# Batched matmul on one core: whole transposes one step ahead, and y loaded two batches per DMA

## The chip, the cores and the metric

One core of one Trainium2 chip. The metric is the device time of one execution in microseconds. Beside it each run gives the core's span (first to last instruction in the records) and the mean clock granted to TensorE.

## The reference

```python
batch, dim_i, dim_j, dim_k = 32, 256, 512, 384      # float32 in and out
out = np.einsum('bij,bjk->bik', x, y)
```

x is 16.8 MB, y 25.2 MB, out 12.6 MB: 54.5 MB to move. The multiplication itself is done in float16 with float32 sums.

## The kernel before

Two batches (G = 2) make a step u, four (Q = 4) a group q of x. One x load of 2 MiB serves two steps. Every load and store is issued from SyncE, in program order (`keep(...)` holds an instruction at its place in the program). The x tiles are transposed on TensorE against an identity (256 transposes), copied out of PSUM as float16 by VectorE and ScalarE, and used as weights.

```python
    def load(u):
        # ... x of the next group, every second step
        y_of[u] = y_pool.tile([P, G, NJ, K], F32, name="y_sb")     # 5 buffers
        for g in range(G):
            keep(nc.sync.dma_start(
                out=y_of[u][:, g],
                in_=y[u * G + g].rearrange("(q t) k -> q t k", q=P)))   # 0.75 MiB, rows of 6,144 bytes

    # ... transpose(q, half): 16 PE transposes, 2 copies on each of VectorE and ScalarE
    # ... round_y(u): 8 casts; multiply(u): 32 matmuls; collect(u): 4 copies out of PSUM

    ahead = LAG - 2                     # LAG = 4
    for u in range(ahead):
        load(u)
    for s in range(U + 2):              # U = 16 steps
        if s + ahead < U:
            load(s + ahead)
        if s == 0:
            transpose(0, 0); transpose(0, 1)
        if s >= 2:
            collect(s - 2)
        if 1 <= s <= U:
            multiply(s - 1)
        if s < U:
            round_y(s)
        for half in range(2):           # first half in step 2q-1, second in step 2q
            q = (s + 1 - half) * G // Q
            if (s + 1 - half) * G % Q == 0 and 0 < q < B // Q:
                transpose(q, half)
        if s >= 2:
            store(s - 2)
```

## Time and profile before

| | before |
|---|---|
| device time, three runs | 135.94, 135.94, 136.25 us |
| span of the profiled run | 134.3 us |
| busiest compute engine | PE, 66% of the span |
| share of the DMA queue | 97.8% |
| last landing of a y batch, issue of the last store, its landing | 124.1, 129.1, 133.4 us |

The page's list of DMA issues tells the shape of the traffic (name, queue, count, size of one, median time from issue to landing):

```profile
y_sb<-in_y_dram SPq DMA_DIRECT2D x32, 768.0 KB, 17.9
x_sb<-in_x_dram SPq DMA_DIRECT2D x8, 2048.0 KB, 20.8
out_dram<-o_sb SPq DMA_DIRECT2D x16, 768.0 KB, 17.8
```

### The profile page before, as it was taken

The page shows a single profiled execution, that of the slowest core. Times are in us where ns is not written, and L with a number is a line of the kernel's source. Part 1 is how long each engine was busy: PE and PEld are TensorE (multiplying, and loading weights), DVE is VectorE, ACT ScalarE, POOL GpSimd, SP SyncE. Part 2 cuts the span into 40 slices and gives each one's busy share as a digit, 9 for nine tenths or more (in the row PEclk, how much of TensorE's full clock was granted, in tenths as well). Part 3 has the DMA queues.
Part 4 walks back from the last instruction along what each step waited for, and adds up shares of the span by engine and source line. Part 5 has one row for each costly group of instructions (what it writes and reads, how often), then busy time and mean ns, then how long its engine had stood idle before and what let it go on. Part 6 is the DMA issues. An engine that isn't in the chain of part 4 may idle for free.

```text
span 134.3 us, 1968 instructions
## 1 busy us (share of the span) xinstructions
PE 88.5 (66%) x768; PEld 73.2 (55%) x768; DVE 56.2 (42%) x128; ACT 63.9 (48%) x129; POOL 0.7 (1%) x6
## 2 busy tenths in 40 slices
PE   0049494979299767786099771976439986597920
PEld 0049474768177666666078661864427665476810
DVE  0004717471743365711634318460363425628620
ACT  3004837662762476712744428560475336738610
POOL 2000000000000000000000000000000000000000
PEclk9999999999959999999968999999965899779997
DMA  5999999999999999999999999999999999999993
GB/s 112 415 400 450 409 417 421 456 388 421 417 448 408 409 428 421 457 394 417 413 443 436 408 417 428 442 422 402 425 423 444 426 402 427 419 427 419 417 394 158
DMA packets 8073, 54.65 MB, mean 407 GB/s; under 512 B 896, under 2 KB 896, under 8 KB 7040
## 3 DMA queue, kind: packets, MB, share of 16 engines
q1 hardware_dynamic: 8064, 54.53, 97.8%
q8 instruction: 6, 0.10, 0.3%
q14 instruction: 3, 0.02, 0.0%
HBM read 41.94 MB, written 12.58 MB: 406 GB/s over the span
## 4 chain that ended last, share of the span: by engine, by line
DMA 78%; PE 13%; ACT 4%; DVE 0%; issue 0%
DMA y_sb<-in_y_dram 40%; DMA x_sb<-in_x_dram 38%; PE o_ps L130 9%; PE t_ps L99 3%; ACT xt_sb L107 2%; ACT y_r L116 1%; ACT o_sb L143 1%; DVE o_sb L145 0%
## 5 line engine op out<-in xcount | busy, mean ns | idle before, releaser
L130 PE MATMUL o_ps<-y_r,xt_sb 128*64 128x384 f16 x512 | 52.4, 364 | 28.5 <-ACT o_sb L143 20.8
L130 PEld LDWEIGHTS <-xt_sb 128*64 128x64 f16 x512 | 39.1, 121 | 38.8 <-issue 22.4
L116 ACT CAST y_r<-y_sb 128x384 f16<-128x384 f32 x64 | 29.5, 514 | 38.7 <-DMA y_sb<-in_y_dram 38.6
L99 PE MATMUL t_ps<-identity,x_sb 128*128 128x128 f32 x256 | 36.9, 301 | 11.4 <-DMA x_sb<-in_x_dram 11.4
L99 PEld LDWEIGHTS t_ps<-identity,x_sb 128*128 128x128 f32 x256 | 34.1, 211 | 16.0 <-issue 16.0
L118 DVE CAST y_r<-y_sb 128x384 f16<-128x384 f32 x64 | 20.0, 356 | 46.7 <-DMA y_sb<-in_y_dram 46.7
L107 ACT CAST xt_sb<-t_ps 128x512 f16<-128x512 f32 x32 | 22.4, 731 | 23.6 <-PE t_ps L99 23.6
L105 DVE CAST xt_sb<-t_ps 128x512 f16<-128x512 f32 x32 | 22.6, 728 | 24.1 <-PE t_ps L99 23.8
L145 DVE COPY o_sb<-o_ps 128x384 f32<-128x384 f32 x32 | 16.3, 544 | 2.1 <-PE o_ps L130 2.1
L143 ACT COPY o_sb<-o_ps 128x384 f32<-128x384 f32 x32 | 13.9, 492 | 1.3 <-PE o_ps L130 1.3
L107 ACT ACT_TABLE_LOAD x1 | 1.3, 1283 | 0.7 <-PEq L192 0.7
masks.py:199 POOL TENSOR_SCALAR_AFFINE_SELECT identity<-identity 128x128 f32<-128x128 f32 x1 | 0.3, 294 | 0.1
masks.py:197 POOL MEMSET identity<- 128x128 f32 x1 | 0.2, 206 | 0.3 <-POOLq L192 0.3
L192 POOL MEMSET const-bfloat16-1.0<- 128x1 bf16 x1 | 0.1, 102 | 0.0
L192 POOL MEMSET const-uint8-127<- 128x1 uint8 x1 | 0.1, 102 | 0.0
L192 POOL MEMSET const-float32-0.0<- 128x1 f32 x1 | 0.1, 99 | 0.2 <-issue 0.2
L192 POOL MEMSET const-float32-1.0<- 128x1 f32 x1 | 0.1, 99 | 0.0
## 6 DMA issues: line engine op xcount, KB each, us to landing
y_sb<-in_y_dram SPq DMA_DIRECT2D x32, 768.0 KB, 17.9
x_sb<-in_x_dram SPq DMA_DIRECT2D x8, 2048.0 KB, 20.8
out_dram<-o_sb SPq DMA_DIRECT2D x16, 768.0 KB, 17.8
```

The lines of the kernel that those rows point to most:

```text
L99: nc.tensor.transpose(t_ps[:, f, h], x_sb[:, h * NE + e + f, t::NJ], identity)
L105: keep(nc.vector.tensor_copy(dst, t_ps))
L107: keep(nc.scalar.copy(dst, t_ps))
L116: keep(nc.scalar.copy(yr_of[u][:, g, t], y_sb[:, g, t]))
L118: keep(nc.vector.tensor_copy(yr_of[u][:, g, t], y_sb[:, g, t]))
L130: nc.tensor.matmul(o_ps[g * M : (g + 1) * M], xt_sb[:, t, e, a * PQ : (a + 1) * PQ].rearrange("c p h -> c (p h)"), y_r[:, g, t], start=(t ...
L143: keep(nc.scalar.copy(o_of[u][:, e], ps_of[u][e]))
L145: keep(nc.vector.tensor_copy(o_of[u][:, e], ps_of[u][e]))
L192: nc = _bacc.Bacc("TRN2", target_bir_lowering=False, num_devices=1)
```

## The change

The intent was to issue fewer and larger loads, and to have all of a group's transposes done a step before they are needed, so that none stands between two multiplications.

```diff
-        for g in range(G):
+        n = 1 if u == U - 1 else G
+        for g in range(0, G, n):
+            b = u * G + g
             keep(nc.sync.dma_start(
-                    out=y_of[u][:, g],
-                    in_=y[u * G + g].rearrange("(q t) k -> q t k", q=P),
+                    out=y_of[u][:, g : g + n],
+                    in_=y[b : b + n].rearrange("g (q t) k -> q g t k", q=P),
 ...
-        for half in range(2):
-            q = (s + 1 - half) * G // Q
-            if (s + 1 - half) * G % Q == 0 and 0 < q < B // Q:
-                transpose(q, half)
+        if (s + 1) * G % Q == 0 and s + 1 < U:
+            transpose((s + 1) * G // Q)
```

(Cut: `transpose(q)` now loops over all NJ tiles; step 0 calls it once.)

More of the change, by code (lines that the diff above doesn't have):

```diff
@@ L78, in load, with transpose @@
         y_of[u] = y_pool.tile([P, G, NJ, K], F32, name="y_sb")
-        for g in range(G):
+        n = 1 if u == U - 1 else G
+        for g in range(0, G, n):
+            b = u * G + g
             keep(
                 nc.sync.dma_start(
-                    out=y_of[u][:, g],
-                    in_=y[u * G + g].rearrange("(q t) k -> q t k", q=P),
-                )
-            )
-    def transpose(q, half):
-        x_sb = x_of[q]
-        if half == 0:
-            xt_of[q] = xt_pool.tile([P, NJ, NE, Q * PQ, H], MM_DT, name="xt_sb")
+                    out=y_of[u][:, g : g + n],
+                    in_=y[b : b + n].rearrange("g (q t) k -> q g t k", q=P),
+                )
+            )
+    def transpose(q):
+        x_sb = x_of.pop(q)
+        xt_of[q] = xt_pool.tile([P, NJ, NE, Q * PQ, H], MM_DT, name="xt_sb")
         n = 0
-        for t in range(half * NJ // 2, (half + 1) * NJ // 2):
+        for t in range(NJ):
             for e in range(0, NE, 2):
@@ L163 @@
         if s == 0:
-            transpose(0, 0)
-            transpose(0, 1)
+            transpose(0)
         if s >= 2:
```

## The prediction

> **What bounds the kernel now.** I read the page from the top: the busy shares, then the slices, then the DMA queue, then the chain that ended last, and last the SyncE queue and the end of the timeline.
>
> ```profile
> PE 88.5 (66%) x768; PEld 73.2 (55%) x768; DVE 56.2 (42%) x128; ACT 63.9 (48%) x129; POOL 0.7 (1%) x6
> ...
> DMA  5999999999999999999999999999999999999993
> ...
> DMA packets 8073, 54.65 MB, mean 407 GB/s; under 512 B 896, under 2 KB 896, under 8 KB 7040
> ...
> q1 hardware_dynamic: 8064, 54.53, 97.8%
> ...
> DMA 78%; PE 13%; ACT 4%; DVE 0%; issue 0%
> ```
>
> No compute engine is busy over 66% of the span; the 16 DMA engines are busy in every slice but the first and the last, and the packets of the one queue take 97.8% of them. So the kernel is bound by moving 54.5 MB. The chain says only 78% DMA because at two places it walks through compute that releases a store; that is not idle DMA, as the slices there still read 9.
>
> The next view asks what the queue of transfers itself waits for (the waits of the SyncE queue):
>
> ```profile
> SPq L81 <- DMA x_sb<-in_x_dram: 32.8, 7, 5.4
> SPq L150 <- DVE o_sb L145: 20.3, 5, 7.1
> SPq L81 <- DMA y_sb<-in_y_dram: 19.7, 13, 1.5
> SPq L150 <- DMA y_sb<-in_y_dram: 16.7, 11, 1.6
> ```
>
> Loads of y (L81) wait for earlier transfers of x and y, and half of the waiting stores (L150) do too. The listing of the built program shows why: each transfer takes one of eight semaphores in turn, and the ninth waits until the first has landed. So eight transfers are in flight, and the page's 17.9 us from issue to landing of y is the length of that queue: eight transfers of 0.97 MB on average (54.5 MB / 56) at 420 GB/s are 18.5 us. The queue is long, and that is good: nothing runs dry.
>
> The end of the timeline (start, length, engine and line) shows the drain:
>
> ```profile
> 123.51 1.77 ACT L116 CAST y_r<-y_sb 128x384 f16<-128x384 f32 x4
> 124.15 0.63 DVE L118 CAST y_r<-y_sb 128x384 f16<-128x384 f32 x2 [0.28 <-DMA y_sb<-in_y_dram]
> ...
> 128.44 0.56 DVE L145 COPY o_sb<-o_ps 128x384 f32<-128x384 f32 x1 [0.74 <-PE o_ps L130]
> ```
>
> The last batch of y lands at 124.15, the last result is copied out at 129.0, the span ends at 134.3. Five stores (11 to 15 in program order) come after that last load: 5 x 0.786 MB / 420 GB/s = 9.4 us, and 124.15 + 9.4 = 133.5. So the DMA drains without a gap of note to the end.
>
> [...] 896 packets under 512 B are 56 transfers x 16. [...] A y load here is 0.75 MiB and becomes 1.5 MiB. [...] with eight queued, slices already run at 388 to 457 GB/s. [...] the packet records of the trace give 234 ns (median) for a 6,144-byte packet and 9 ns for a semaphore write, so a batch of y is 8 x 234 + 9 = 1.88 us on its engine, and the landings of stores and y batches in the end phase are 1.8 to 1.9 us apart[...].
>
> **The change part by part.**
> *y in pairs.* 32 loads become 17 (15 pairs, and two single ones at the end). Bytes, 6,144-byte rows and the order of x, y and stores on the SyncE queue stay. Removed: 15 semaphore writes per engine, 15 x 9 ns = 0.135 us, on the bound; and 15 issues of 0.33 us, 5 us of SyncE's time, which nothing waits for. Also eight transfers now hold more bytes (54.5 / 41 = 1.33 MB each), so the eight semaphores stop being the limit of the queue and the stores' waits become it. Check that the queue cannot run dry: a y load is issued once the store five steps of y before it in program order is ready. By the timeline that store follows its own multiply; I put it at most 6 us after the landing of the next pair of y, four steps before the load in question lands. A step moves 54.5 / 16 = 3.4 MB, 8.2 us; four steps are 33 us, less 6, less 3.7 for the load itself, leaves over 20 us of work queued ahead. No gap.
> Against it: a pair lands as one, so the casts of its first batch start about 1.9 us later; ACT must then do four casts (4 x 0.514 = 2.06 us) after the landing and not two (1.03): +1.0 us on the compute side of a step.
> *Transposes.* 256 transposes, 64 copies out of PSUM: same count, same sizes, so nothing is removed. The second half of a group of four batches moves from just before its own multiply to one step earlier, so odd steps carry 32 transposes and 8 copies, even ones none. In an odd step, 16 more transposes (2.2 us) and two more copies on each of ACT and DVE (2 x 0.73) stand between the casts and the collecting of the last result: some 2 us later there. In the next step the same 2.2 us + 0.7 us wait is gone. x has landed well before, as it is queued ahead of that step's y. Compute per two steps stays 88.5 / 8 = 11 us of PE against 16.4 us of DMA.
> *The tail.* Before, at 119.95 the last 16 transposes hold multiply 14 up until 123.01. After, by the durations of that timeline: pair 13 lands at 113.0, four ACT casts to 115, copies and transposes to about 117.8, first collect copy 118.3, multiply 13 to 121.0 (2.75 us at full clock) or 122.8 (4.47 us, as that stretch had), multiply 14 behind it, multiply 15 from about 125.1, when the last y is rounded, to 127.8. So the last store is issued near 128.4 where it was 129.1. But the DMA has stores 11 to 14 to move until 131.6 anyway, so those 0.7 us are hidden, but for the small dip in the queue just before 129.1, worth 0.1 us at most.
> *Sum.* The densest reading of the trace: x of the first group lands at 8.59 us; then 48 transfers of 1.881 us and seven of x at 8 x 611 + 9 ns = 4.90 us make 124.6 us, so 133.2, and the last landing, read from the semaphore records, is 133.4. There is 0.2 us of slack in the whole kernel. After the change: -0.135 -0.05 (chosen) gives about -0.2 us: 135.94 becomes **135.75 us**.
>
> **The rivals.**
> (a) *Fewer, larger DMAs are really faster* [...]: if each removed transfer saved a bubble of 0.2 us, 3 us, 133 us. Against: 1.88 us per batch is the sum of its packets; no room for a bubble.
> (b) *The tail turns compute-bound*: with PE at half clock through multiplies 13 to 15 (4.47 us each) the last would end near 131 to 132, the last store be issued at 132 and land some 3.5 us later: 135.5 for the span in place of 134.3, so 137.1. For it: the granted clock was 0.76 from 113 to 120 us. Against: from 120 to 134 it was near full, and the denser transposes come earlier.
> (c) *Pairs read two places of y in turn, 0.79 MB apart*, in place of one run; packets could get slower. 1% more per y packet is 0.6 us. Nothing in the trace speaks for it, as packet length is unchanged; it could go either way.
> (d) *A dry queue at the start*: store 0 now comes after all transposes of group 1, about 26 us in place of 23.9. By then 13 loads (now 8) of 14.2 MB are queued, good until 35 us. No loss.
>
> **Range and chances.** The runs of before differ by 0.3 us (135.94 to 136.25); (c) and the noise give about 0.5 either way, (b) a thin tail upward: 135.2 to 136.4. Over 2% either way means more than 2.7 us: only (a) or a strong form of (b) or (c) reach it. Same 0.96, faster 0.02, slower 0.02.
>
> **What would show it.** Packets under 512 B fall from 896 to 656; the queue's share stays near 98%; the median y landing grows from 17.9 us to over 20; SyncE's waits of L81 on earlier transfers shrink and its stores' waits on o_sb grow; the last y still lands at about 124; no slice of DMA between the first and the last two falls under 9. I am wrong if slices show holes (b, d), or if 6,144-byte packets have another median than 234 ns (a, c).

Its sum: -0.135 -0.05 = -0.185 us, so 135.94 becomes 135.75. What its figures rest on: the 420 GB/s is the rate in the trace (414 to 431 GB/s in each stretch from 8.6 to 127 us). The 56 landings fall on eight semaphores in turn, seven on each; the first transfer landed at 8.59 us and the ninth was issued at 8.60. The trace has 896 packets of 4 bytes, and as many increments of these eight semaphores: the "semaphore writes". The multiply of 4.47 us ran at a mean clock of 0.62 (116 to 120 us), so not at half clock throughout; a multiply at full clock took 2.79 us there, where the forecast estimates 2.75. The bubble of 0.2 us in rival (a) and the 3.5 us from issue to landing in rival (b) were assumptions; later runs measured 3.6 and 3.2 us for the second.

## The result, and the profile after

The changed kernel took **136.50 us** (median of six, 136.30 to 136.72) and the kernel before, in six runs (the three above among them), 136.22 us (135.94 to 136.33). The ratio is 1.0024, 95% interval 1.0009 to 1.0039: the same within 2%, as forecast, but 0.1 us above the range of 135.2 to 136.4, and on the slow side of 1 where the prediction was on the fast side. Ratios here are the mean time of one kernel's fast runs over that of the other's of the same rounds, so not quite the ratio of the medians quoted.

The page after, the lines that answer to those of the prediction (DMA busy by slice, packets, the queue's share, the chain that ended last):

```profile
PE 88.7 (66%) x768; PEld 76.1 (57%) x768; DVE 56.2 (42%) x128; ACT 62.4 (46%) x129; POOL 0.7 (1%) x6
...
DMA  5999999999999999999999999999999999999993
...
DMA packets 7833, 54.64 MB, mean 407 GB/s; under 512 B 657, under 2 KB 657, under 8 KB 6801
...
q1 hardware_dynamic: 7824, 54.53, 97.7%
...
DMA 72%; PE 11%; DVE 6%; SPq 3%; issue 2%; ACT 1%; DVEq 0%; ACTq 0%
```

Nothing that bounds the kernel moved. The 240 small packets that went from the queue (8,064 to 7,824) are 15 transfers x 16 semaphore writes; the bytes, the mean rate of 407 GB/s and the full slices are the same.

What SyncE's queue waits for, after:

```profile
SPq L152 <- DVE o_sb L147: 91.7, 16, 17.5
SPq L84 <- DMA x_sb<-in_x_dram: 4.6, 4, 1.7
SPq L202 <- DMA out_dram<-o_sb: 4.1, 1, 4.1
```

and the list of issues, after:

```profile
y_sb<-in_y_dram SPq DMA_DIRECT2D x15, 1536.0 KB, 24.3
...
y_sb<-in_y_dram SPq DMA_DIRECT2D x2, 768.0 KB, 18.7
```

The loads hardly wait for an earlier transfer any more; the stores wait for their results instead, 91.7 us in all. This large change of who waits for whom cost nothing, because the queue stays 24 us long. The end of the timeline after:

```profile
118.90 5.50 PE L132 MATMUL o_ps<-y_r,xt_sb 128*64 128x384 f16 x64 [0.40 <-DVE o_sb L147]
...
124.27 0.63 DVE L120 CAST y_r<-y_sb 128x384 f16<-128x384 f32 x2 [1.13 <-DMA y_sb<-in_y_dram]
...
128.25 0.56 DVE L147 COPY o_sb<-o_ps 128x384 f32<-128x384 f32 x1 [0.74 <-PE o_ps L132]
```

Multiplications 13 and 14 (64 matmuls) now run back to back in 5.50 us, and end at 124.40 as the last y lands (its casts start at 124.27); before, transposes lay between these two. The last store is issued at 128.87 and not 129.08, and lands at 133.40 and not 133.43. So inside the queue the two kernels end within 0.03 us of each other. The 0.3 us has to be looked for behind the last landing.

### The profile page after: what moved, and what is told of

Same layout as the page of the kernel before. It is cut to its first block, busy times and chain, and to the rows that moved or that the text cites. A ratio compares the mean times of both kernels' runs of the same rounds, so it can differ in the third digit from the quotient of the medians.

```text
span 134.3 us, 1957 instructions
## 1 busy us (share of the span) xinstructions
PE 88.7 (66%) x768; PEld 76.1 (57%) x768; DVE 56.2 (42%) x128; ACT 62.4 (46%) x129; POOL 0.7 (1%) x6
## 3 DMA queue, kind: packets, MB, share of 16 engines
q1 hardware_dynamic: 7824, 54.53, 97.7%
## 4 chain that ended last, share of the span: by engine, by line
DMA 72%; PE 11%; DVE 6%; SPq 3%; issue 2%; ACT 1%; DVEq 0%; ACTq 0%
DMA y_sb<-in_y_dram 72%; PE t_ps L101 6%; PE o_ps L132 5%; DVE y_r L120 3%; DVE xt_sb L107 2%; SPq L84 2%; DVE o_sb L147 2%; SPq L66 1%; ACT o_sb L145 1%; SPq L152 0%; ACT xt_sb L109 0%; DVEq L120 0%; DVEq L147 0%; ACTq L145 0%
## 5 line engine op out<-in xcount | busy, mean ns | idle before, releaser
L101 PE MATMUL t_ps<-identity,x_sb 128*128 128x128 f32 x256 | 44.2, 342 | 33.0 <-DVE xt_sb L107 21.1
L101 PEld LDWEIGHTS t_ps<-identity,x_sb 128*128 128x128 f32 x256 | 40.5, 215 | 36.8 <-DVE xt_sb L107 22.5
L132 PE MATMUL o_ps<-y_r,xt_sb 128*64 128x384 f16 x512 | 44.7, 331 | 6.4 <-DVE o_sb L147 4.8
L118 ACT CAST y_r<-y_sb 128x384 f16<-128x384 f32 x64 | 28.2, 520 | 42.9 <-DMA y_sb<-in_y_dram 42.8
L132 PEld LDWEIGHTS <-xt_sb 128*64 128x64 f16 x512 | 35.6, 112 | 15.0 <-issue 6.6
L120 DVE CAST y_r<-y_sb 128x384 f16<-128x384 f32 x64 | 18.6, 354 | 43.1 <-DMA y_sb<-in_y_dram 43.0
L147 DVE COPY o_sb<-o_ps 128x384 f32<-128x384 f32 x32 | 17.0, 550 | 8.4 <-PE o_ps L132 8.2
## 6 DMA issues: line engine op xcount, KB each, us to landing
y_sb<-in_y_dram SPq DMA_DIRECT2D x15, 1536.0 KB, 24.3
```

What stands on the lines that cost most here:

```text
L101: nc.tensor.transpose(t_ps[:, f, h], x_sb[:, h * NE + e + f, t::NJ], identity)
L118: keep(nc.scalar.copy(yr_of[u][:, g, t], y_sb[:, g, t]))
L120: keep(nc.vector.tensor_copy(yr_of[u][:, g, t], y_sb[:, g, t]))
L132: nc.tensor.matmul(o_ps[g * M : (g + 1) * M], xt_sb[:, t, e, a * PQ : (a + 1) * PQ].rearrange("c p h -> c (p h)"), y_r[:, g, t], start=(t ...
L147: keep(nc.vector.tensor_copy(o_of[u][:, e], ps_of[u][e]))
```

## The experiments

**Two theories.** Theory A: the 0.24% is a cost inside the queue of transfers, from y read at two places in turn, from the longer queue, or from the transposes. Theory B: it lies outside what the queue does, at the end of the program or beyond the span, or is drift. By the 2% rule every kernel below is the same as the one before, but for one transfer more (unclear) and y in partition halves (slower); the smaller differences are read from the intervals, the spans and the traces. Later runs were told apart by two finer theories, L (order of the closing waits) and T (the end of the compute). Kernels are compared only within the same rounds. A quantity that turned out useful is *device time minus span*; call it the outside time.

### The same program again

A comment was added to the kernel before; the instruction lists are the same.

> The kernel before, unchanged but for a comment, as a measure of the noise. Theory A (the recorded 0.24% of the change is a real cost inside the transfers' queue) and theory B (it is a cost outside the span that the profile covers, or drift between runs) both want a ratio of 1.000 within 0.0015; if this run alone is off by 0.002, the 0.0024 of the change is no more than noise.

Measured: 136.32 us, ratio 1.0024 (1.0012 to 1.0037). The very same program, loaded again, shows the ratio of the change. The interval covers the runs of one load of the program, not the difference between loads. So a ratio of 1.0024 alone proves nothing here. But the parts differ: this run's spans are 134.4 to 134.8 us (those of the kernel before in the same rounds 134.1 to 134.4), its outside time is 1.79 us on average, as theirs, 1.81.

### Each half of the change alone

```diff
 (y pairs only)        y loads as in the change; transpose(q, half) as before
 (transposes only)     y loads as before; transpose(q) as in the change
```

> Only the y loads in pairs, the transposes as before. The prediction's own term: 15 semaphore writes of 9 ns fewer per engine, -0.14 us, ratio 0.999. If reading two places of y in turn or the longer queue is what costs (theory A, y half), +0.3 us, ratio 1.002, with more packets above 234 ns. Median landing of y about 24 us and not 17.9.

> Only the transposes all in the step ahead, y loaded one batch at a time. If the transposes cause the 0.3 us (theory A, compute half), ratio 1.002 and a later last store; the prediction's term is -0.05 us, ratio 0.9996, as the queue of transfers never runs dry. Median landing of y stays near 18 us.

> The whole change again. Theory A: ratio 1.0024 within 0.0015 as recorded. If the recorded ratio was drift or noise: 0.999 to 1.001. Span of the profile 134.3 to 134.5 us either way.

Measured, with the kernel before of the same rounds (11 runs, 135.99 us):

| | median us | ratio (95%) | mean span | mean outside time |
|---|---|---|---|---|
| before | 135.99 | | 134.21 | 1.81 |
| y pairs only | 136.49 | 1.0040 (1.0019 to 1.0062) | 134.47 | 2.10 |
| transposes only | 135.98 | 1.0009 (0.9987 to 1.0030) | 134.35 | 1.79 |
| change again | 136.30 | 1.0028 (1.0015 to 1.0040) | 134.32 | 2.06 |

The change repeats: +0.36 us on the means, of which 0.11 in the span and 0.25 outside it. The outside time goes with the y half and not with the transposes. The transposes alone are neutral: five of their six runs have spans of 134.1 to 134.3, one 135.1, to which we come back.

Where do the 0.11 us in the span come from? From the last landing to the end of the span there are 0.835 us before and 0.933 us after, by the semaphore records of both traces; the pairs alone have 0.934, the transposes alone 0.835. That is reproducible to a few ns. The records show why: at the end SyncE asks the eight semaphores of the transfers (and two others) in five instructions of two each, 62 to 83 ns apart when nothing is waited for. With 56 transfers the last store has a semaphore of the last of the five. With 41 it has one of the third; SyncE sits 4.0 us in that wait (the 4.1 us of L202 above) and then still has two more instructions to ask. The view of these lines, before and after (duration in ns: least, median, most; then first and last start), shows the one long wait; before, the waits stand in front of such instructions and none inside one:

```profile
L203 SPq EVENT_SEMAPHORE  x7: 17/28/28, 129.8 to 134.2; - x7
...
L202 SPq EVENT_SEMAPHORE  x7: 17/27/4035, 129.2 to 134.3; - x7
```

### Is it the order of the closing waits? (theory L)

```diff
 (one transfer more: kernel before, one y load of the middle cut in two)
+            w = P // 2 if u == U // 2 and g == 0 else P
+            for p in range(0, P, w):
                 keep(nc.sync.dma_start(out=y_of[u][p : p + w, g], ...[p : p + w]))
 (half the pairs: the change, singles in the second half)
-        n = 1 if u == U - 1 else G
+        n = 1 if u >= U // 2 else G
```

> The kernel before with one y load of the middle cut in two by partitions: 57 transfers, so the last store has the first of the eight semaphores, as with the 41 of the change (before: 56, the eighth). Theory L (the change's cost is at the end of the program: the last transfer's semaphore is no longer the one that the closing waits ask last): 0.93 us from the last landing to the end of the span, as the change has, in place of 0.83, and 2.0 to 2.1 us of device time outside the span in place of 1.8; ratio 1.001 to 1.003. Theory P (it comes with the pairs themselves): 0.83 us, 1.8 us, ratio 1.000 to 1.001.

> The change with pairs only in the first half of the batches: 48 transfers, so the last store has the eighth semaphore again. Theory L: 0.83 us from the last landing to the end of the span and 1.8 us outside it, ratio 0.999 to 1.000. Theory P: 0.93 us and about 1.95 to 2.1 us, ratio 1.001 to 1.0025.

Measured for one transfer more: 0.939 us from the last landing to the end, as theory L said, with single y loads and the old transposes. So these 0.1 us are the closing waits. But the outside time was 1.81 us: that part of theory L fell. And the ratio was 1.0206 (1.0175 to 1.0238), far above what either theory allowed: one load out of 32, cut by partitions, cost 2.8 us. The views of both kernels over the stretch where it lies (stretch, its length, then busy time of PE, PEld, DVE, ACT and POOL, then clock, DMA share, GB/s), first this kernel:

```profile
64.00:80.00 16.00, 10.69 (x91) 8.71 (x91) 6.40 (x14) 7.11 (x15) 0.00 (x0) 0.89 1.01 381
```

and the kernel before:

```profile
64.00:80.00 16.00, 11.51 (x96) 9.41 (x96) 7.04 (x16) 7.85 (x17) 0.00 (x0) 0.89 1.01 424
```

The DMA share is full in both (1.01), yet 381 GB/s are moved in place of 424: the engines are as busy and slower.

Half the pairs (48 transfers): 136.27 us, ratio 1.0012 (0.9995 to 1.0028), outside time 1.82 us on average, so without the extra. But 1.094 us from the last landing to the end, where 0.83 was expected: one of SyncE's last instructions starts 0.46 us after the one ahead of it, before 0.09. A quarter of a microsecond (1.094 less 0.835) that was outside with 41 transfers now shows inside the span; whether it is the same one is taken up below.

### What a y load cut by partitions costs

```diff
 (y in partition halves: kernel before)
+            w = P // 2
+            for p in range(0, P, w):
                 keep(nc.sync.dma_start(out=y_of[u][p : p + w, g], ...[p : p + w]))
```

> The kernel before with every y load cut in two by partitions: 88 transfers, same packets of 6,144 bytes, 32 more semaphore writes per engine and half the bytes in flight per y load. If a transfer costs its 9 ns write and nothing else: +0.29 us, ratio 1.002, last landing about 133.7. If each transfer also costs a bubble (rival a of the prediction, 0.2 us each): +6 us. Median landing of y 11 to 13 us, as eight transfers now hold 5 MB.

It was meant to measure the price of 32 more semaphore writes. It measured something else: a median of 183.15 us over all six runs, and ratio 1.2915 (1.2872 to 1.2958) on the two fast ones (175.3 and 176.4 us). Every number of the expectation missed; the median y landing was 17.6 us. Its page, from a run in the slow state (185.0 us) and so only for the shape (GB/s by slice, then packets):

```profile
GB/s 175 366 235 362 275 236 234 333 302 223 243 342 418 207 322 307 416 292 239 379 351 420 218 298 287 390 341 219 311 282 439 294 238 320 274 307 287 373 204 180
DMA packets 8585, 54.65 MB, mean 299 GB/s; under 512 B 1408, under 2 KB 1408, under 8 KB 7552
```

The packets of 6,144 bytes are the same in number and size; their median went from 234 to 348 ns. In its page the queue's packets fill 96.8% of the 16 engines' time, and the rate swings between 207 and 439 GB/s in the slices between the ends. Why packets of the same size took longer is not shown by any trace here. The run says nothing on the price of a semaphore write, and the experiment above with one cut load is spoilt as a time, perhaps in the same way (its 6,144-byte packets took 92.25 us in sum per engine, before 90.56); its two readings behind the last landing stand. Why one cut load cost 2.8 us, and 32 together only 1.2 us each on the fast runs, stays open.

### Pairs or number of transfers?

```diff
 (all pairs: the change with)                 n = G
 (tiny loads: the change with, behind each pair)
+        if u < U - 1:
+            keep(nc.sync.dma_start(out=tiny[:, u], in_=y[0, u*16:(u+1)*16, 0:8]))   # never used
 (pairs in the second half: the change with)  n = 1 if u < U // 2 else G
```

> The change with the last two y batches paired too: 40 transfers, so the last store has the eighth semaphore. Theory L: 0.83 us from the last landing to the end of the span. If the 2.0 to 2.2 us outside the span belongs to programs with nearly all y in pairs: again 2.0 to 2.2; if it belonged to the order of the closing waits: 1.8. The last pair lands whole, so its first casts start 1.9 us later and the last store is issued near 129.8, where 129.0 was free: +0.1 to +0.3 us in the span. Ratio 1.002 to 1.004.

> The change with one tiny load (16 rows of 32 bytes, never used) behind each pair: 56 transfers again, pairs kept. If the time outside the span goes with the number of transfers on the queue: 1.8 us. If with the pairs: 2.0 to 2.2 us. The span grows by up to 1.5 us (15 more packets and semaphore writes per engine), 0.83 us from the last landing to its end (theory L).

> Pairs in the second half of the batches only, the last two included: 48 transfers. If the time outside the span goes with the number of transfers: 1.8 us as with pairs in the first half. If with what the program ends with: 2.0 to 2.2 us. 0.83 us from the last landing to the end (theory L); ratio 1.000 to 1.003.

| kernel | transfers | last landing to end of span | mean outside time | ratio (95%) |
|---|---|---|---|---|
| before | 56 | 0.835 | 1.80 to 1.81 | |
| all pairs | 40 | 0.830 | 2.07 | 1.0028 (1.0013 to 1.0043) |
| change, first measured | 41 | 0.933 | 2.08 | 1.0024 (1.0009 to 1.0039) |
| pairs in the first half | 48 | 1.094 | 1.82 | 1.0012 (0.9995 to 1.0028) |
| pairs in the second half | 48 | 1.098 | 1.80 | 1.0018 (1.0003 to 1.0032) |
| change with tiny loads | 56 | 0.834 | 1.83 | 1.0010 (0.9996 to 1.0023) |

All pairs has the last store on the last semaphore again, and the 0.1 us is gone (0.830) while the 2.07 us stays: the two costs are separate. (In its one trace the last store was issued at 129.80, as expected, and landed 0.3 us later than before.) Both kernels with 48 transfers missed the 0.83 us of theory L. The tiny loads settle whose the outside time is. They keep every pair and add 15 useless transfers, and the outside time falls back to 1.83 us, the end to 0.834. **So the quarter of a microsecond goes with the number of transfers that the program issues, not with the pairs.** The span of that kernel grew by 0.09 us on the means (134.38 against 134.29) for 15 tiny transfers; the 1.5 us of the expectation was the author's assumption, and no run shows it.

The traces show where such a quarter can come from. Count SyncE's recorded instructions (transfers, waits, drains) from the start of a trace. In front of the 80th stands a pause of 0.41 to 0.46 us in ten of the eleven traces that have an 80th, whatever instruction that is. Five of them, and the change:

| kernel | transfers | SyncE instructions | the pause, us | what comes after it |
|---|---|---|---|---|
| before | 56 | 89 | 129.41 to 129.83 | a closing wait; the last store lands at 133.43 |
| change with tiny loads | 56 | 89 | 129.58 to 130.01 | a closing wait; the last store lands at 133.81 |
| one transfer more | 57 | 90 | 131.33 to 131.79 | issue of the last store |
| pairs in the first half | 48 | 81 | 133.53 to 133.97 | a closing drain, behind the last landing |
| pairs in the second half | 48 | 81 | 133.57 to 134.02 | the same |
| change, all pairs | 41, 40 | 74, 73 | none recorded | the records end before the 80th |

Elsewhere such instructions commonly follow one another in 0.03 to 0.12 us. (Pauses of 0.3 to 0.5 us stand in other places too, but at no other place in all ten traces; in the eleventh trace, y in partition halves, the place lies in a wait of 9.2 us.) With 56 transfers the pause ends before the last store has landed and costs nothing; with 48 it lies in the closing instructions, and 0.26 us of it reach the end of the span. With 40 or 41 it would lie behind the span. The DMA records do reach that far: each trace at 56 or 57 transfers has one packet of 8,192 bytes on the queue that the profile calls `instruction` between 129.9 and 133.7 us; at 48 it starts at 134.6 and 134.7, and at 40 or 41 at 136.3 to 137.0 in four traces of six, some 2 us behind the end of the span (in the other two it is not recorded). So that the place is set by the count of instructions, and with it by the number of transfers, is shown by these ten traces; that the pause behind the span makes the 0.25 us is argued, as no SyncE instruction is recorded there. Two things do not fit or are not explained: three of the 33 runs at 40 or 41 transfers have an outside time of 1.74 to 1.80 us, and the six at 88 have 1.89 to 2.10.

### Is the tail of the compute really hidden? (theory T)

In the transposes-alone set one run took 136.97 us, and it was the profiled one. Its last multiplication and last copy:

```profile
125.56 4.45 PE L130 MATMUL o_ps<-y_r,xt_sb 128*64 128x384 f16 x32 [2.58 <-DVE o_sb L145]
...
130.04 0.56 DVE L145 COPY o_sb<-o_ps 128x384 f32<-128x384 f32 x1 [2.00 <-PE o_ps L130]
```

4.45 us for 32 matmuls in place of 2.79: the clock records have a half-clock stretch of 3.4 us from 126.5. The last store was issued at 130.7 and landed at 134.3, 3.6 us later: the DMA had run out of stores (from 128 to 131 us its share was 0.62 at 260 GB/s, in the kernel before 0.95 at 393). Inside the kernels, half-clock stretches last 3.41 or 6.83 us in the clock records of the kernel before and of the change, and they fall at other places in other runs (from 115.6 us in the kernel before, from 114.3 in its repeat, from 126.5 here). The expectations call such a stretch a half-clock window. The repeat of the kernel before shows the same kind of delay: half clock from 114.3 to 121.1, last store issued at 129.98, landing at 133.88. Its stretch around multiplication 13:

```profile
114.00:121.00 7.00, 5.51 (x33) 3.66 (x33) 2.98 (x8) 3.67 (x8) 0.00 (x0) 0.52 1.02 423
```

and that of the change when run again, with as slow a clock:

```profile
114.00:121.00 7.00, 5.42 (x28) 4.69 (x30) 5.17 (x12) 5.12 (x11) 0.00 (x0) 0.52 1.01 424
```

There the last store was still issued at 128.95. So by this one pair of runs the change buys about a microsecond at the last store when the clock is low there, and 0.2 us otherwise; that its transposes do it is read from the timelines, not tested alone. Two ways to test it: give the tail more room, or less.

```diff
-LAG = 4
+LAG = 5      # transposes of the change, single y loads; and again, loaded anew
+LAG = 5      # the whole change
+LAG = 3      # the whole change
```

> The transposes of the change, single y loads, and every load issued one step earlier, so that six stores and not five follow the last y. Theory T (the single long runs, like 136.97 of the transposes alone and 136.5 of the kernel before, are runs in which a half-clock window lies in the last multiplies and the last store is issued after 129.5 us): the last store is issued near 127.5, no run above 136.2, median 135.8 to 135.95, ratio 0.998 to 0.9995. If the spread is not from the tail: single runs above 136.3 as before.

> The kernel with single y loads, transposes ahead and loads one step earlier, loaded anew. Theory T: again no run with a span above 134.4 us, ratio 0.998 to 1.000. If the first 0.9985 was luck of that load of the program: spans up to 134.8 as in the runs of the kernel before, ratio 1.000 to 1.003.

> The change with every load issued one step earlier. Theory T: last store issued by 129.0 even in a run whose half-clock windows fall late, no run with a span above 134.5. Theory L: still 0.93 us from the last landing to the end, as 41 transfers leave the last store on the first semaphore. Ratio 0.999 to 1.002.

> The change with every load issued one step later, so four stores follow the last y instead of five. Theory T (the end of the compute is hidden only as long as the stores that wait outlast it): the last y lands 1.9 us later, near 126.1, the last store is issued near 131 and lands 3.6 us later, 134.6: +1.2 us, ratio 1.007 to 1.012. If the tail of the compute is not what sets the end: ratio 1.002.

| kernel | median us | ratio (95%) | spans of its runs |
|---|---|---|---|
| LAG 5, transposes ahead, single y | 135.96 | 0.9985 (0.9971 to 0.9999) | 134.1 to 134.2 |
| the same, loaded anew | 135.89 | 0.9984 (0.9972 to 0.9996) | 134.0 to 134.3 |
| LAG 5, the whole change | 136.41 | 1.0028 (1.0009 to 1.0046) | 134.1 to 134.3, one 134.9 |
| LAG 3, the whole change | 137.27 | 1.0086 (1.0071 to 1.0101) | 135.0 to 135.5 |

The kernels before of those rounds had spans up to 134.8 and 134.6. The first LAG 5 run happened to have a half-clock stretch at the very place that hurt above:

```profile
123.37 4.47 PE L130 MATMUL o_ps<-y_r,xt_sb 128*64 128x384 f16 x32 [2.62 <-DVE o_sb L145]
...
127.88 0.56 DVE L145 COPY o_sb<-o_ps 128x384 f32<-128x384 f32 x1 [1.98 <-PE o_ps L130]
```

The same slow multiplication of 4.47 us, and the span was 134.1 us and not 135.1: with six stores behind the last y, the last one, issued at 128.9, still finds the queue busy (DMA share 0.94 at 390 GB/s from 128 to 131 us). This version came out 0.15% below the kernel before, in two loads. That is less than the 0.24% between two loads of one program, so a gain on the kernel before is not shown; nor do eleven runs without a long one prove much, as 18 of the 22 runs of the kernel before in the same rounds stayed at 134.4 us or less too. What the traces show is that the slow multiplication was hidden here and not there. With the change's loads, LAG 5 keeps an outside time of 2.15 us, 0.933 us from the last landing to the end (as theory L said) and ratio 1.0028. One expectation there missed: one run of it had a span of 134.9 with the last store issued at 127.2, so not every long run comes from the tail.

LAG 3 goes the other way. The last y lands at 126.3, then:

```profile
127.45 2.79 PE L132 MATMUL o_ps<-y_r,xt_sb 128*64 128x384 f16 x32 [0.77 <-DVE o_sb L147]
...
130.29 0.56 DVE L147 COPY o_sb<-o_ps 128x384 f32<-128x384 f32 x1 [0.74 <-PE o_ps L132]
```

Last store at 130.9, landing at 134.1; the span grew by 0.9 us on the means (135.20 against 134.32; 1.2 was expected, and 0.1 of the 0.9 is the closing waits) at full clock from 121 us on. The compute is hidden up to a last store at about 129.1 (landing 133.4, with the queue still feeding it) and shows at 130.

### The slow first packets

```diff
 (LAG 5, transposes ahead, single y; first batch of y ahead of the first x)
-        if u == 0:
-            load_x(0)
 ...     # and after the first y load:
+            if u == 0 and g == 0:
+                load_x(0)
```

> The kernel with transposes ahead and loads one step earlier (ratio 0.9985), with the first batch of y ahead of the first group of x. If the slow first packets (1.0 to 2.0 us for 16,384 bytes in place of 0.61) are slow because large ones start together, small ones of 6,144 bytes lose less: up to 0.6 us gained, ratio 0.994 to 0.997. If the first requests are slow whatever their size: the same 1.2 us is lost, ratio 0.998 to 1.000.

Measured: 136.57 us, ratio 1.0039 (1.0017 to 1.0061), a miss. The stretches of this kernel:

```profile
0.00:10.00 10.00, 0.00 (x0) 0.00 (x0) 0.00 (x0) 1.28 (x1) 0.70 (x6) 1.00 0.82 331
...
40.00:48.00 8.00, 5.82 (x62) 4.89 (x58) 1.67 (x5) 2.44 (x7) 0.00 (x0) 1.00 0.98 371
```

and of its base, x first:

```profile
0.00:10.00 10.00, 1.32 (x7) 1.36 (x8) 0.19 (x1) 1.28 (x1) 0.70 (x6) 1.00 0.82 309
...
40.00:48.00 8.00, 7.46 (x80) 6.32 (x79) 4.20 (x12) 5.16 (x14) 0.00 (x0) 1.00 0.98 403
```

The start did gain, 22 GB/s over 10 us, worth 0.5 us at 424 GB/s. It was given back between 40 and 48 us (32 GB/s over 8 us, 0.6 us), where 33 of 462 packets of 6,144 bytes took 350 to 600 ns in place of 234 (none of 464 did in its base). Why there stays open.

## Why the prediction was right or wrong

**What bounds the kernel: right.** The queue of transfers is full in both kernels (97.8% and 97.7%), and the last landing of the changed one is within 0.03 us of the other's.

**The queue cannot run dry: right.** Median y landing rose to 24.3 us (over 20 forecast), stores waited 91.7 us for results, no slice has a hole, the last y lands at 124.2. At the start (rival d) store 0 was issued at 26.8 us (about 26 forecast) and nothing ran dry.

**15 semaphore writes, -0.135 us: right for the engines, lost in the time.** Summed over the packet records, semaphore writes took 0.506 us per engine before and 0.371 after, exactly the term. But the sum of the data packets varies as much between traces (in these two the 6,144-byte ones took 0.09 us per engine more, the 16,384-byte ones 0.07 less), and the slowest engine's last landing did not move. Over runs the span did not shrink.

**The tail: right that it is hidden; the -0.05 us did not show.** The last store was issued 0.2 us earlier (forecast 0.7) and landed 0.03 us earlier. Rival (b), the compute-bound tail, was seen in single runs of the kernel before and of the transposes alone, where a half-clock stretch lay in multiplication 13 or in the last one; at LAG 3 the spans of all runs (135.0 to 135.5) show it.

**Rivals (a) and (c): neither.** No bubble per transfer: y batches and stores land 1.81 to 1.93 us apart after 120 us, before and after, and their packets and one write come to 1.88; the median packet stayed at 234 ns. Rival (c) can't be ruled out below some 0.2 us: the pairs alone had a mean span 0.26 us longer, half of it from one run of 135.1 and 0.10 from the closing waits.

**The sum: wrong, and here is the step that failed.** "After the change: -0.135 -0.05 (chosen) gives about -0.2 us" treats everything behind the last landing as constant. It was not. Two terms were missing: +0.10 us for the closing waits, because 41 transfers leave the last store on a semaphore that is asked two instructions before the end, and +0.25 to 0.28 us of device time outside the span, which the runs tie to the number of transfers. Together 0.35 to 0.38 us, which is the measured difference (0.33 us on the means of the first measurement, 0.36 of the repeat); the -0.185 us is not to be seen beside it. Every sign that the prediction named came true and the number was still outside the range, because the signs watch the queue and the cost lies behind it. The closing waits stand in the trace of the kernel before and in the built program, so the first term could have been worked out; of the second that trace shows the pause in front of the 80th instruction, but not that it would cost anything elsewhere.

**The range: too narrow at its base.** It was built around 135.94, the median of three runs. Over later rounds the same kernel gave medians of 135.99 to 136.22, and one loaded anew 136.32. With 136.1 as base and the two missing terms, 136.5 is where one lands.

**Readings that were off without harm.** Of the sixteen waits of stores in the lines that it shows eleven, and not half, were for an earlier y. Four casts on ACT took 1.77 us (the first line of its timeline), not 2.06.

## What to carry to other kernels

When one queue of transfers is full from the first slice to the last, larger loads and better ordered compute moved nothing but waits here (407 GB/s with either); ask instead what lies before the first byte and behind the last landing. The number of transfers had effects there that have nothing to do with bandwidth: which semaphore the last one gets (0.1 us), and where a pause in SyncE's instructions falls (0.26 us inside the span at 48 transfers; that it is also the 0.25 us outside the span at 41 is argued, not shown). If compute follows the last load, keep enough stores queued behind it to cover a half-clock stretch (3.4 us here), here six and not five; and before believing a ratio of 1.002, run the same program again.
